# Emptying the q and k banks of attention with ScalarE alone, and splitting them from SBUF

## The chip, the cores and the metric

The kernel runs on one core of a Trainium2 chip. Its engines are TensorE (PE, with the weight load PEld beside it), VectorE (DVE), ScalarE (ACT), GpSimd (POOL) and the DMA queues that SyncE (SP) and ScalarE issue to. The metric is the device time of one execution in microseconds, lower is better. The output must agree with the reference.

## What is computed

The reference is an encoder of two layers on 1024 tokens of width 1024. Each layer multiplies the normalised input with one combined matrix and hands the columns to three mixers: a convolution module, differential attention and a gated delta rule. What matters here, cut from it:

```python
h = rms_norm(x, ...)
u = h @ W_in                       # one projection, its columns go to the three mixers
# differential attention: 6 heads, two softmax maps for each
qf = q.reshape(..., 2 * H, 32) * 32 ** -0.5
s  = einsum("bqmd,bkmd->bmqk", qf, kf)
p  = softmax(s - slopes * |t - s|)
a  = p[:, :, 0] - lam * p[:, :, 1]
# gated delta rule, in chunks of 64
A   = where(strict, (kb @ k^T) * decay, 0)
sol = triangular_solve(A, rhs, lower=True, unit_diagonal=True)
y = concat(A, B, C) @ W_out ;  x = x + rms_norm(y)
x = x + rms_norm(relu(rms_norm(x) @ W1)^2 @ W2)
```

## The kernel before

**Products.** Every dense product in fp32 is made from three matmuls of a rounded type (mm3, L163 to L165): each operand is held as a high part (the value rounded) and a low part (the rest), and high*high, high*low and low*high are summed in a PSUM bank. `split` makes the parts from a tile in SBUF: ScalarE copies it to the high part (L168), VectorE subtracts that from the tile (L169). `load_split` loads a slice of a weight by SP (L177) and splits it (tiles wr, wh, wl).

**The stage.** In each layer the product with W_in runs as a list of column slices, `dense_fm` for each: 128 columns by 1024 tokens, as two halves of 512 tokens, each half 24 matmuls into one of three banks named at, and then a function that empties the bank. `dense_fm` runs that function under a high priority. `attqk(w, j)` is the slice of attention's q (w = 0) or k (w = 1), pair j of three: ScalarE writes the high part qkh from the bank (L425 with the scale for q, L428 for k), and VectorE the low part qkl from the bank and qkh (L426, L429). Then three DMAs of 512 KB write them to DRAM (L434): two of qkh from ScalarE's queue, one of qkl from SP's. There are 2 layers x 2 x 3 = 12 calls, and 24 halves.

**Beside it** runs the delta rule's triangular inverse, `invert`, once for each p = 0, 1, 2 in a layer, as a generator of which pieces are woven into the list of slices. SP loads the blocks (tiles Lr and Lp, L776), ScalarE transposes half of them (L777), GpSimd does 31 steps of substitution, a product and a difference in each (L787 to a tile subt, L788 to Xm), ScalarE transposes the result (L790, XT), SP stores it to xi (L792, L793) and loads its blocks (Ta and Tt, L801, L804), and PE makes the blocks off the diagonal from them (L811, L819). The results (kta) are stored and loaded again for the scan. VectorE in the meantime does the convolution (L508, L512, accumulators ca), and small parts of the delta rule.

**The stage behind** is attention, with the scan woven in. Its first matmuls (L1068) take a stack of q and k that SP loads from DRAM (tile stkE, L1038, three loads), then that of the next block (stk).

**The order** of each engine's instructions is set when the kernel is built: the program gives the operations and their priorities, and a scheduler that estimates when each could run puts them in a row, engine by engine. A change of one operation therefore also moves others. At run time each engine works through its row in order and waits where an operand isn't there.

Of the kernel before, what the change touches and what calls it, by code (L numbers as in the profile page):

```python
# [9 lines left out]
F32 = mybir.dt.float32  # L10
F32R = mybir.dt.float32r
BF16 = mybir.dt.bfloat16
AF = mybir.ActivationFunctionType
ALU = mybir.AluOpType
# [64 lines left out]
class K:  # L79
# [213 lines left out]
    def w_in_phase(self, l, L):  # L293
        nc, a, tc = self.nc, self.a, self.tc
        win = a["w_in"][l].rearrange("(c p) n -> p c n", p=P)
        hTh, hTl = self.hT
        with tc.tile_pool(name=f"wA{l}", bufs=1, reuse_waits=RW) as W:

            def tmp(name, dt=F32, n=S):
                return W.tile([P, n], dt, tag="tmp", bufs=self.TB, name=name)  # L300
# [83 lines left out]
            with tc.tile_pool(name=f"gt{l}", bufs=1, side="right", reuse_waits=RW) as gp:  # L384
                ps = self.rot_bank()[:, 0:NT * 48].rearrange("p (t x) -> p t x", x=48)
# [30 lines left out]
            def attqk(w, j):  # L416
                col = (C_DQ, C_DK)[w] + j * P
                th = tmp(f"qkh{l}_{w}_{j}", F32R)
                tl = tmp(f"qkl{l}_{w}_{j}", F32R)
                qs = self.C["qs"][:, j:j + 1]  # L420

                def ev(n, ps):
                    sl = slice(512 * n, 512 * n + 512)
                    if w == 0:
                        nc.scalar.activation(th[:, sl], ps, AF.Copy, scale=qs)  # L425
                        nc.vector.scalar_tensor_tensor(tl[:, sl], ps, qs, th[:, sl].bitcast(F32), ALU.mult, ALU.subtract)  # L426
                    else:
                        nc.scalar.activation(th[:, sl], ps, AF.Copy)  # L428
                        nc.vector.tensor_tensor(tl[:, sl], ps, th[:, sl].bitcast(F32), op=ALU.subtract)  # L429

                self.dense_fm(win[:, :, col:col + P], ev)
                for b in range(3):
                    lo = b == 2 - (w == 0)
                    (nc.sync if lo else nc.scalar).dma_start(self.qk[j, b, :, w], (tl if lo else th).bitcast(F32))  # L434
# [13 lines left out]
            for j in range(3):  # L448
                todo += [lambda j=j: attqk(0, j), lambda j=j: attqk(1, j)]
# [1185 lines left out]
```

## Time and profile before

| | us |
|---|---|
| median of 3 runs | 2913.32 |
| lowest and highest | 2912.23, 2919.48 |
| the profiled execution | 2917.9 |
| its span in the trace | 2916.1 |

The stages in the trace: the product with W_in of layer 0, then from 409.04 us on attention and the scan, then the product with W_out and the MLP; layer 1 repeats this, with its attention from 1864.51 us on. A row of a timeline reads: start, duration, engine, line, operation, output <- inputs, shape, and in brackets how long the engine was idle before it and what ended that.

### The profile page before, as it was taken

What the parts mean: (1) busy time and instruction counts of PE and PEld (TensorE: products, weight loads), DVE (VectorE), ACT (ScalarE), POOL (GpSimd) and SP (SyncE); (2) the same over time, 40 slices, a digit from 0 to 9 for tenths busy, and PEclk for the clock granted to TensorE, in tenths of its full rate; (3) what the DMA queues carried; (4) which work ended last, traced back from release to release, by engine and by line L of the source; (5) the groups of instructions that cost most, each with busy time, mean ns of one, the idle gap of its engine ahead of it and who ended that gap; (6) DMA issues with size and microseconds to landing.
All of it is one profiled execution on the core that took longest, in us unless ns stands there. A gap on an engine that the chain in (4) does not pass through costs nothing.

```text
span 2916.1 us, 46184 instructions
## 1 busy us (share of the span) xinstructions
PE 2681.5 (92%) x17292; PEld 2155.4 (74%) x17292; DVE 2064.0 (71%) x3781; ACT 1404.8 (48%) x2468; POOL 842.7 (29%) x793
## 2 busy tenths in 40 slices
PE   8987989888999998999999879698889999989997
PEld 7865766666888886888787667476668888868886
DVE  5797247987488776777768871388874977757776
ACT  5433336586356664322554332276853566643224
POOL 2289636754100000000112985377530000000000
PEclk9998989989999999999999989799989999999999
DMA  5467795433235558655445496953332455586643
GB/s 133 151 172 210 219 225 145 117 102 123 87 105 216 206 192 314 233 202 184 150 118 146 142 265 170 224 150 107 109 121 75 145 196 206 212 336 209 220 169 116
DMA packets 415314, 504.76 MB, mean 173 GB/s; under 512 B 125401, under 2 KB 313945, under 8 KB 412786
## 3 DMA queue, kind: packets, MB, share of 16 engines
q1 hardware_dynamic: 359362, 373.92, 42.9%
q10 hardware_dynamic: 55728, 127.88, 11.5%
q8 instruction: 137, 2.24, 0.3%
q14 instruction: 87, 0.71, 0.1%
HBM read 318.01 MB, written 182.12 MB: 172 GB/s over the span
## 4 chain that ended last, share of the span: by engine, by line
PE 62%; POOL 11%; DMA 10%; DVE 8%; issue 4%; ACT 2%; SPq 2%; ACTq 0%; DVEq 0%; POOLq 0%
PE at L163 10%; PE at L164 10%; PE at L165 10%; PE sc L163 4%; PE sc L164 4%; PE sc L165 4%; POOL Xm L788 4%; POOL subt L787 3%; DVE sc L1070 3%; PE dt L163 2%; PE dt L164 2%; PE dt L165 2%; PE tr L163 2%; PE tr L164 2%; DMA qkT<-gq 2%
## 5 line engine op out<-in xcount | busy, mean ns | idle before, releaser
L158 POOL TENSOR_TENSOR pro<-pr,mhalf 128x1 f32<-128x1 f32 x32 | 18.5, 578 | 1417.8 <-DVE pr L207 1415.0
L163 PE MATMUL at<-hTh,wh 128*128 128x512 f32 (+1 forms) x832 | 326.8, 394 | 11.8 <-DVE qkl L426 8.0
L165 PE MATMUL at<-hTh,wl 128*128 128x512 f32 (+1 forms) x832 | 325.5, 392 | 5.4 <-DVE wl L169 5.4
L164 PE MATMUL at<-hTl,wh 128*128 128x512 f32 (+1 forms) x832 | 326.3, 392 | 0.0
L1073 ACT ACTIVATE sc<-sc,mx 128x1024 f32<-128x1024 f32 x192 | 220.2, 1149 | 94.3 <-DVE mx L1070 89.1
L163 PEld LDWEIGHTS at<-hTh,wh 128*128 128x128 f32 x832 | 160.3, 193 | 43.4 <-DVE qkl L426 8.5
L165 PEld LDWEIGHTS at<-hTh,wl 128*128 128x128 f32 x832 | 160.3, 193 | 37.2 <-DVE wl L169 6.2
L164 PEld LDWEIGHTS at<-hTl,wh 128*128 128x128 f32 x832 | 160.6, 193 | 31.0 <-issue 0.8
L1068 PE MATMUL at<-stk 96*128 96x512 f32 x352 | 153.7, 489 | 29.7 <-DVE mx L1070 27.9
L1070 DVE CUSTOM_DVE_ANT_0 sc<-at,bias 128x512 f32<-128x512 f32 x192 | 129.7, 684 | 43.0 <-PE at L1068 25.0
L1070 DVE CUSTOM_DVE_ANT_0 sc<-at,bias,mx 128x512 f32<-128x512 f32 x192 | 141.9, 745 | 19.6 <-PE at L1068 13.8
L1180 ACT ACTIVATE ob<-sb 128x512 fp32r<-128x512 f32 x120 | 74.8, 626 | 155.0 <-PE tr L165 54.8
L169 DVE TENSOR_TENSOR wl<-wr,wh 128x1024 fp32r<-128x1024 f32 x48 | 65.2, 1359 | 117.5 <-ACT wh L168 117.4
L787 POOL TENSOR_TENSOR subt<-Lp,Xm 128x31 f32<-128x31 f32 (+15 forms) x186 | 124.9, 672 | 70.9 <-DMA Lp<-ai 50.5
L163 PE MATMUL at<-ob,oa 128*128 128x512 f32 x356 | 138.4, 391 | 2.1 <-ACT at L1508 2.1
L164 PE MATMUL at<-ob,oa 128*128 128x512 f32 x356 | 138.6, 390 | 0.0
L165 PE MATMUL at<-ob,oa 128*128 128x512 f32 x356 | 138.0, 389 | 0.0
L788 POOL TENSOR_TENSOR Xm<-Xm,subt 128x31 f32<-128x31 f32 (+15 forms) x186 | 133.9, 720 | 12.9
L1094 PE MATMUL tr<-consts,sc 128*128 128x128 f32 x704 | 114.8, 296 | 15.3 <-DVE sc L1090 4.6
L1180 ACT ACTIVATE ob<-w2r 128x512 fp32r<-128x512 f32 x92 | 57.6, 629 | 130.7 <-PE tr L165 52.1
L1094 PEld LDWEIGHTS tr<-consts,sc 128*128 128x128 f32 x704 | 85.7, 150 | 36.9 <-issue 11.4
L1068 PEld LDWEIGHTS at<-stk 96*128 96x128 f32 x352 | 66.0, 203 | 61.2 <-DVE mx L1070 48.9
(469 smaller groups left out, 7940.2 us busy)
## 6 DMA issues: line engine op xcount, KB each, us to landing
hd<-oa ACTq DMA_DIRECT2D x120, 512.0 KB, 6.3
oa<-hd SPq DMA_DIRECT2D x120, 512.0 KB, 4.4
w1r<-in_w_ff_dram SPq DMA_DIRECT2D x32, 1024.0 KB, 5.6
w2r<-in_w_ff_dram SPq DMA_DIRECT2D x64, 512.0 KB, 7.1
wr<-in_w_in_dram SPq DMA_DIRECT2D x50, 512.0 KB, 4.8
ld<-hd SPq DMA_DIRECT2D x98, 256.0 KB, 3.9
kta<-kta SPq DMA_DIRECT2D x32, 576.0 KB, 9.9
stk<-qk SPq DMA_DIRECT2D x66, 256.0 KB, 5.0
```

Source lines behind the costliest of these rows:

```text
L158: self.nc.gpsimd.tensor_tensor(out, x, half[:, :n], op=ALU.pow)
L163: mm(ps, lhsT=lh, rhs=rh, start=first, stop=False, skip_group_check=more)
L164: mm(ps, lhsT=lh, rhs=rl, start=False, stop=False, skip_group_check=more)
L165: mm(ps, lhsT=ll, rhs=rh, start=False, stop=last, skip_group_check=more)
L169: (eng or self.nc.vector).tensor_tensor(lo, raw, hi.bitcast(F32), op=ALU.subtract)
L787: nc.gpsimd.tensor_tensor(tv, Lp[:, j + 1:, j:j + 1].broadcast_to([P, n, w]), Xm[:, j:j + 1, 0:w].broadcast_to([P, n, w]), op=ALU.mult)
L788: nc.gpsimd.tensor_tensor(Xm[:, j + 1:, 0:w], Xm[:, j + 1:, 0:w], tv, op=ALU.subtract)
L1068: mm(ps, lhsT=st[:, 0, t * P:(t + 1) * P], rhs=st[:, 1, ks], start=True, stop=True)
L1070: nc.vector.tensor_tensor_reduce(out=sc[:, ks], in0=ps, in1=self.bias[:, o:o + 512], scale=slope, scalar=mx[:, 0:1] if n2 else 3.0e38, op0 ...
L1073: nc.scalar.activation(sc, sc, AF.Exp, scale=-1.0, bias=mx[:, 1:2], accum_out=oS[:, t, mp:mp + 1])
L1094: nc.tensor.transpose(ps[:, k], pp[0][:, (4 * q + k) * P:(4 * q + k + 1) * P], self.ident)
L1180: self.nc.scalar.activation(h, src, AF.Copy)
```

## The change

`attqk` no longer writes both parts from the bank. ScalarE copies each half to the tile qkl as plain fp32 (with the scale for q), and that is all that reads the bank. Behind the two halves, outside of the high priority, `split` is called on the whole tile: ScalarE makes qkh from qkl in SBUF (L168, 128x1024), and VectorE overwrites qkl with qkl minus qkh (L169, 128x1024). The DMAs stand behind that.

```diff
 def ev(n, ps):
     sl = slice(512 * n, 512 * n + 512)
-    if w == 0:
-        nc.scalar.activation(th[:, sl], ps, AF.Copy, scale=qs)
-        nc.vector.scalar_tensor_tensor(tl[:, sl], ps, qs, th[:, sl].bitcast(F32), ALU.mult, ALU.subtract)
-    else:
-        nc.scalar.activation(th[:, sl], ps, AF.Copy)
-        nc.vector.tensor_tensor(tl[:, sl], ps, th[:, sl].bitcast(F32), op=ALU.subtract)
+    nc.scalar.activation(tl[:, sl].bitcast(F32), ps, AF.Copy, scale=1.0 if w else qs)

 self.dense_fm(win[:, :, col:col + P], ev)
+self.split(tl.bitcast(F32), th, tl)
 for b in range(3):
```

`split`, which it calls, is unchanged:

```python
def split(self, raw, hi, lo, eng=None):
    self.nc.scalar.activation(hi, raw, AF.Copy)
    (eng or self.nc.vector).tensor_tensor(lo, raw, hi.bitcast(F32), op=ALU.subtract)
```

The scheduler moves other instructions too, in the latter part of each W_in stage and in both attention stages; the MLP keeps its order. Three places follow. The changed kernel's line numbers are four lower behind the edit. A name such as Lp0_2 is layer 0, p = 2; qkl0_0_2 is layer 0, q, pair 2.

ScalarE's row in layer 0, from the transpose behind p = 1 (XT0_1) to that ahead of p = 2 (Lp0_2), before:

```order
L790 ACTIVATE XT0_1_1729<-Xm0_1_1728 128x1024
L537 ACT_TABLE_LOAD
L537 ACTIVATE yo0_0_3033<-sc1133_3011,conv_ln_b_347,conv_ln_w_345 128x256 x2
L538 DMA yd_76<-yo0_0_3033 128x256 x2
L425 ACTIVATE qkh0_0_2_3187<-at149_3222,consts_63 128x512
L168 ACTIVATE wh153_3319<-wr153_3318 128x1024
L434 DMA qk_75<-qkh0_0_2_3187 128x1024 x2
L777 ACTIVATE Lp0_2_2377<-Lr0_2_2376 64x1024
```

and in the changed kernel:

```order
L786 ACTIVATE XT0_1_1729<-Xm0_1_1728 128x1024
L533 ACT_TABLE_LOAD
L533 ACTIVATE yo0_0_3033<-sc1133_3011,conv_ln_b_347,conv_ln_w_345 128x256 x2
L534 DMA yd_76<-yo0_0_3033 128x256 x2
L168 ACTIVATE wh153_3319<-wr153_3318 128x1024
L424 ACTIVATE qkl0_0_2_3188<-at149_3221,consts_63 128x512
L168 ACTIVATE qkh0_0_2_3187<-qkl0_0_2_3188 128x1024
L430 DMA qk_75<-qkh0_0_2_3187 128x1024 x2
L773 ACTIVATE Lp0_2_2377<-Lr0_2_2376 64x1024
```

One more copy of 128x1024 stands ahead of the transpose, and the two DMAs of qkh are issued behind it.

SP's queue in layer 1, between p = 1 and p = 2 (xi1 is where p = 1 is stored, Lr1_2 the blocks that p = 2 starts from, wr1735 a weight slice), before:

```order
L792 DMA xi1_80<-Xm1_1_15135 128x1024
L793 DMA xi1_80<-XT1_1_15136 128x1024
L177 DMA wr1735_16945<-in_w_in_dram 128x8x128
L776 DMA Lr1_2_15783<-ai0_77 16x32x32 x4
L646 DMA vs_83<-vs1_1_1_15843 128x4x128
L434 DMA qk_75<-qkl1_0_2_16595 128x1024
```

and in the changed kernel:

```order
L788 DMA xi1_80<-Xm1_1_15135 128x1024
L772 DMA Lr1_2_15783<-ai0_77 16x32x32 x2
L177 DMA wr1735_16945<-in_w_in_dram 128x8x128
L789 DMA xi1_80<-XT1_1_15136 128x1024
L772 DMA Lr1_2_15783<-ai0_77 16x32x32 x2
L430 DMA qk_75<-qkl1_0_2_16595 128x1024
```

Two of the four loads of Lr now stand ahead of the store of XT and of the weight slice.

SP's queue in layer 0 at the start of attention (stkE0 is the first stack of q and k, stk0_0_1 the second, vtE0 the first block of v), before:

```order
L1038 DMA stkE0_3384<-qk_75 32x2048 x3
L476 DMA vtE0_3385<-av_74 128x1024
L743 DMA eg0_2_3693<-eg_85 64x3x128
L1038 DMA stk0_0_1_4303<-qk_75 32x2048 x3
L743 DMA eg0_2_3693<-eg_85 64x3x128
```

and in the changed kernel:

```order
L1034 DMA stkE0_3384<-qk_75 32x2048
L1034 DMA stk0_0_1_4303<-qk_75 32x2048 x3
L1034 DMA stkE0_3384<-qk_75 32x2048 x2
L472 DMA vtE0_3385<-av_74 128x1024
L739 DMA eg0_2_3693<-eg_85 64x3x128 x2
```

The three loads of the second stack now stand between the first load and the last two of the first stack.

## Rows read from the trace of the kernel before

**Rows 1.** The page: busy time of each engine, and shares of the chain by engine.

```profile
PE 2681.5 (92%) x17292; PEld 2155.4 (74%) x17292; DVE 2064.0 (71%) x3781; ACT 1404.8 (48%) x2468; POOL 842.7 (29%) x793
...
PE 62%; POOL 11%; DMA 10%; DVE 8%; issue 4%; ACT 2%; SPq 2%; ACTq 0%; DVEq 0%; POOLq 0%
```

**Rows 2.** Tile qkl: who waited for it (us, times), in the whole execution.

```profile
  PE at L163: 8.0, 1
```

**Rows 3.** Timeline of PE: two places in layer 0's W_in stage, and the first attention matmuls.

```profile
230.89 0.80 PE L163 MATMUL at<-hTh,wh 128*128 128x512 f32 x1 [8.05 <-DVE qkl L426]
...
236.29 0.31 PE L811 MATMUL dt<-Ta,Ao 32*32 32x32 f32 x2 [3.75 <-DMA Ta<-xi]
...
409.04 1.19 PE L1068 MATMUL at<-stkE 96*128 96x512 f32 x2 [6.65 <-DMA stkE<-qk]
...
415.65 0.73 PE L1068 MATMUL at<-stk 96*128 96x512 f32 x2
```

**Rows 4.** Timeline of ScalarE: layer 0 at 227 and 301 us, layer 1 at 1755 us.

```profile
227.27 1.97 ACT L790 ACTIVATE XT<-Xm 128x1024 f32<-128x1024 f32 x1 [15.42 <-POOL Xm L788]
229.14 0.68 ACT L425 ACTIVATE qkh<-at,consts 128x512 fp32r<-128x512 f32 x1
...
301.07 1.05 ACT L168 ACTIVATE wh<-wr 128x1024 fp32r<-128x1024 f32 x1
...
303.36 2.12 ACT L777 ACTIVATE Lp<-Lr 64x1024 f32<-64x1024 f32 x1 [1.23 <-DMA Lr<-ai]
...
1755.08 2.11 ACT L777 ACTIVATE Lp<-Lr 64x1024 f32<-64x1024 f32 x1 [2.35 <-DMA Lr<-ai]
```

**Rows 5.** Timeline of VectorE: layer 0's W_in stage, five places.

```profile
230.10 0.74 DVE L426 SCALAR_TENSOR_TENSOR qkl<-at,consts,qkh 128x512 fp32r<-128x512 f32 x1
...
248.09 1.51 DVE L169 TENSOR_TENSOR wl<-wr,wh 128x1024 fp32r<-128x1024 f32 x1
...
314.24 1.22 DVE L169 TENSOR_TENSOR wl<-wr,wh 128x1024 fp32r<-128x1024 f32 x1 [6.77 <-ACT wh L168]
315.98 0.68 DVE L429 TENSOR_TENSOR qkl<-at,qkh 128x512 fp32r<-128x512 f32 x1
...
325.53 1.65 DVE L169 TENSOR_TENSOR wl<-wr,wh 128x1024 fp32r<-128x1024 f32 x1 [4.19 <-ACT wh L168]
```

**Rows 6.** Timeline of GpSimd: the substitution at the same places, and layer 1's at 1766 us.

```profile
247.70 0.82 POOL L787 TENSOR_TENSOR subt<-Lp,Xm 128x156 f32<-128x156 f32 x1
248.60 1.36 POOL L788 TENSOR_TENSOR Xm<-Xm,subt 128x156 f32<-128x156 f32 x1
...
305.61 0.26 POOL L787 TENSOR_TENSOR subt<-Lp,Xm 128x31 f32<-128x31 f32 x1 [0.68 <-ACT Lp L777]
...
314.29 1.63 POOL L788 TENSOR_TENSOR Xm<-Xm,subt 128x207 f32<-128x207 f32 x1
...
316.00 0.60 POOL L787 TENSOR_TENSOR subt<-Lp,Xm 128x220 f32<-128x220 f32 x1
...
324.69 0.69 POOL L788 TENSOR_TENSOR Xm<-Xm,subt 128x255 f32<-128x255 f32 x1
...
326.17 1.60 POOL L788 TENSOR_TENSOR Xm<-Xm,subt 128x256 f32<-128x256 f32 x1
...
1766.50 0.60 POOL L788 TENSOR_TENSOR Xm<-Xm,subt 128x207 f32<-128x207 f32 x1
```

**Rows 7.** Timeline of SP, the time to issue: attention's start, and Lr in layer 1.

```profile
396.09 3.29 SPq L1038 DMA_DIRECT2D stkE<-qk  x3
...
401.93 3.72 SPq L1038 DMA_DIRECT2D stk<-qk  x3
...
1746.84 4.83 SPq L776 DMA_DIRECT2D Lr<-ai  x4
```

**Rows 8.** Windows of attention: PE, PEld, DVE, ACT, POOL busy, then clock, DMA share, GB/s.

```profile
409.00:500.00 91.00, 82.19 (x997) 60.87 (x999) 68.98 (x185) 59.89 (x114) 52.43 (x38) 0.91 0.69 176
500.00:600.00 100.00, 90.38 (x1080) 68.58 (x1077) 89.80 (x229) 63.86 (x125) 65.00 (x44) 0.91 0.41 106
```

## The prediction

> **What bounds the kernel now.** I read the page first: PE is busy 92% of the span and holds 62% of the chain, but GpSimd, busy 29%, holds 11% [rows 1]. A chain that leaves the busiest engine is where a small change can count, so the next view was the chain in order of time. In the tail of each W_in stage, which is where the twelve calls of `attqk` stand, it runs through GpSimd's substitution (L787, L788), from there to ScalarE's transposes (L790, L777), to SP's stores and loads, and so to the first stack of attention. PE has slack there: the first attention matmul of layer 0 waits 6.65 us for stkE [rows 3]. So a microsecond that PE gains in this tail is worth nothing, and one that the substitution or SP's queue loses is paid. Then I asked who waits for what the change removes (rows 2), and looked at what runs at the same time on VectorE and GpSimd (rows 5 and 6).
>
> **The wait that goes.** The edit takes VectorE out of the release of 24 banks. In the whole execution PE waits for VectorE's eviction once, for 8.0 us [rows 2], at 230.89 us [rows 3]. But VectorE is not why: ScalarE had waited 15.42 us for the substitution to be done, transposed it until 229.24, and only then wrote qkh, until 229.82; VectorE read the bank at 230.10 and was done at 230.84 [rows 4, 5]. With the edit PE starts at about 229.9, 1.0 us earlier. Three matmuls later it stops again, for 3.75 us, on Ta [rows 3], which comes from SP and not from the banks; in the changed row of PE that wait still stands three dense matmuls behind. So the 1.0 us goes into the next wait: **0**, at most -1.0. Nobody else waits for these evictions.
>
> **ScalarE's new copies.** Twelve copies of 128x1024 at 1.05 us (the nearest row is the same operation on a weight, from SBUF to SBUF [rows 4]) are 12.6 us; the 24 evictions stay at about their 0.68. ScalarE is busy 48% [rows 1], and these copies wait for nothing that is late, so most is hidden by idle time. The exception is layer 0 between p = 1 and p = 2: the order shows one copy more ahead of L777, which starts at 303.36 behind the copy of 301.07 and its DMAs [rows 4], and GpSimd starts p = 2 as soon as L777 is through [rows 6]. L777 had waited 1.23 us for Lr, but the copy and two issues behind it end at about 304.6: **+1.2** (between 0 and +1.2: the lower end if the eviction ahead of it comes sooner). That is also what a cover gone would cost elsewhere: 1.05 us a copy.
>
> **VectorE's own time.** 24 operations of 0.74 (q, 12) and 0.68 (k, 12) go [rows 5], 17.0 us. Twelve of L169 come; undisturbed one takes 1.22, among GpSimd's work 1.51 to 1.65 [rows 5], so 14.6 to 19.8 us. That is nothing either way, and what waits for it, a store of qkl, isn't wanted before attention begins: stkE is issued at 396.09 [rows 7].
>
> **What the new form does to GpSimd.** This is the main term. L169 reads two tiles in SBUF; L426 and L429 read one and a bank. In the trace the two kinds differ in what they do to the operation of GpSimd beside them:
> - with the L169 of 314.24, L788 on 128x207 takes 1.63; the same shape takes 0.60 in layer 1, where VectorE is idle [rows 5, 6]: 1.03 more;
> - with that of 325.53, 128x256 takes 1.60; its neighbour of 128x255 takes 0.69: 0.91 more;
> - in p = 1, where VectorE's convolution (two tiles in SBUF as well) already holds GpSimd up, with that of 248.09 an operation takes 1.36 against 0.82 for its neighbour: 0.54 more;
> - beside L429 at 315.98, L787 on 128x220 takes 0.60: nothing more [rows 5, 6].
>
> So operations free for GpSimd become ones that hold it. By the order, nine of the twelve splits fall on a substitution: four on p = 1 and one on p = 2 in layer 0, three and one in layer 1. At 0.54 for the seven in p = 1 and 0.95 for the two in p = 2 this is 3.8 + 1.9 = **+5.7**. The bounds are 0, if the splits land in the gaps in which GpSimd waits, and 9 x 1.03 = +9.3. I take the rows of the stage that each split lies in.
>
> The Trainium skill speaks against the change here: its page "SBUF — State Buffer", section "Who interferes with whom", says that a VectorE instruction with two SBUF inputs contends with a GpSimd instruction that reads SBUF, one with at most one such input doesn't, and that the lock is exclusive. The trace agrees on who contends (1.63 against 0.60); if GpSimd stood still for the whole of each split, the sum would be that of the first rival below.
>
> **What is moved on SP.** Layer 1, before p = 2: L777 waits 2.35 us for Lr [rows 4], whose four loads take 4.83 us to issue [rows 7]. Two of them now stand ahead of XT's store, in time in which SP waited for ScalarE, so the rest ends up to 2.4 us sooner; ScalarE's row has L777 earlier too. **-2.0**, between -2.4 and 0. Layer 0, at attention's start: three loads of the second stack, 3.72 us of issuing [rows 7], stand ahead of two of the first. The first attention matmul, which waits for stkE [rows 3], can be up to 3.7 later, but the second stack, wanted at 415.65 [rows 3], is then there already, and the scheduler's store ahead of it on ScalarE comes earlier. **+1.0**, between 0 and +3.7, nearer the lower end since PE's work behind the second stack catches up.
>
> **Attention's order.** Both attention stages are reordered as a side effect, with the same operations. No row prices this. VectorE is busy 68.98 of 91.00 us at the start of layer 0's attention, and 89.80 of 100.00 later [rows 8], so the start holds (0.898 - 0.758) x 91 = 12.7 us of idle time more than steady work does. A better order could win back at most that much, and a worse one lose about as much as SP's term above, 3.7 a layer. I take **0**, as the same work meets the same bound.
>
> **The sum.** -0 (bank) + 1.2 (ScalarE) + 5.7 (GpSimd) - 2.0 + 1.0 (SP) + 0 (order) = +5.9 us. The profiled execution of 2917.9 would become 2923.8; it lies 4.6 above the median, 2913.3, and the comparison is with the median: 2913.3 + 5.9 = **2919**.
>
> **Rivals.**
> 1. *The lock is dearer.* If GpSimd stands still for a whole split, each of the nine costs an average of the 1.22, 1.51 and 1.65 seen [rows 5], 1.46: 13.1 instead of 5.7, so +13.3, **2927**. For it: 1.03 was lost with a split of 1.22. Against it: 0.91 with one of 1.65. It decides the sign that can be measured from (8.7 - 0.2) / 9 = 0.94 us a split on. The rule of the Trainium skill's page "SBUF — State Buffer" would give this.
> 2. *The start of attention gets faster.* Its new order fills VectorE's extra idle time, 12.7 us in layer 0 [rows 8], with none counted for layer 1: -12.7, and +0.2 for the tail's other terms with the splits in gaps, **2901**. For it: attention begins with stacks that come late [rows 3], and the order of loads there has changed. Against it: nothing in the edit makes them come sooner.
> 3. *The change doesn't do what it says.* The banks were released late by ScalarE's queue and not by VectorE [rows 4], so nothing is gained; and the splits land in GpSimd's gaps, so nothing is lost: **2913**. For it: one wait in the whole execution [rows 2]. Against it: GpSimd has few gaps in p = 1.
>
> **How the numbers follow.** About 0.3%, 8.7 us, is what a measurement of this kernel can tell from no change. My forecast, +5.9, with its own range of 2911 to 2927, has 0.40; of that 0.12 lies above 2922. Rival 1 has 0.20, all of it slower. Rival 2 has 0.28, of which 0.04 within the bound. Rival 3 has 0.12. So faster 0.24, same 0.28 + 0.04 + 0.12 = 0.44, slower 0.12 + 0.20 = 0.32. The range for 8 in 10 reaches from 2902, which leaves out about 0.12 of rival 2, to 2931, which is rival 1 with SP's two terms at their upper ends and leaves out under 0.08.
>
> **What would show it.** In the changed trace: no wait of PE for tile qkl, and a wait of about 7 us at the same place, now for ScalarE (the bank step); GpSimd operations beside an L169 on qkl longer by 0.5 to 1.0 us, p = 1 and p = 2 longer by 2.2 and 0.9 us in layer 0 (the main term); GpSimd's p = 2 starting 1.2 us later after the end of p = 1 in layer 0 and 2 us sooner in layer 1; the first attention matmul of layer 0 some 5 us later than 409.04. I am wrong if the substitutions keep their lengths, or if attention itself, from its first matmul to the last, changes by more than 4 us in either layer: then the order and not the edit made the time.

## The result and the profile after

The change makes the kernel slower. Four runs of it have a median of 2935.7 us (2931.75 to 2941.1) against 2914.94 for four of before (2912.23 to 2919.48). The two medians are 20.8 us apart; the ratio on record, 1.0065 with a 95% interval of [1.0048, 1.0082], makes it some 19 us, and that is what is used below. The forecast was 2919, and 2935.7 lies above the range of 2902 to 2931. The profiled execution of the changed kernel took 2941.1 us, with a span of 2939.3; that is 23.2 more than the span before. Line numbers of the changed kernel are four lower behind the edit, so that L1066 there is L1070 of before.

The page's busy times, and its chain by engine, to be read against [rows 1]:

```profile
PE 2688.7 (91%) x17292; PEld 2160.6 (74%) x17292; DVE 2080.8 (71%) x3769; ACT 1417.8 (48%) x2480; POOL 852.8 (29%) x793
...
PE 63%; DMA 10%; POOL 10%; DVE 9%; issue 4%; ACT 2%; SPq 1%; ACTq 0%; DVEq 0%; POOLq 0%
```

The counts are as the diff says: 12 operations fewer on VectorE, 12 more on ScalarE. But VectorE is busy 16.8 us longer, where 17.0 us of evictions went out and at most 19.8 came in: 14 us more than the edit's own, so some other work of VectorE got longer.

Where the time appears is seen on PE. Its first attention matmul is at 417.02 in layer 0 (409.04 before, [rows 3]) and at 1874.49 in layer 1 (1864.51 before); the transposes that end attention are at 719.65 (709.32) and 2182.49 (2157.33). So the changed kernel is 8.0 us late when attention of layer 0 begins, 10.3 when it ends, 10.0 when attention of layer 1 begins and **25.2 when that ends**. Layer 1's attention alone is 15.2 us longer, though it holds the same operations. The windows of it, of before and then of after (length, busy us of PE, PEld, DVE, ACT and POOL with their counts, granted clock, DMA share, GB/s):

```profile
1864.51:2157.33 292.82, 257.62 (x2752) 189.83 (x2753) 248.08 (x625) 200.75 (x390) 186.25 (x113) 0.92 0.43 120
```

```profile
1874.49:2182.49 308.00, 262.85 (x2753) 194.56 (x2753) 261.99 (x625) 201.76 (x390) 188.41 (x113) 0.91 0.42 115
```

VectorE does the same 625 operations in 262.0 instead of 248.1 us. PE is not busy for 45.2 us instead of 35.2. What it waits for there stands in the view of PE's waits (engine, line, what it waited for: us in total, times, longest), of before and then of after:

```profile
PE at L1068 <- DVE mx L1070: 11.7, 15, 5.0
...
PE tr L1094 <- POOL sc L1088: 3.6, 1, 3.6
```

```profile
PE at L1064 <- DVE mx L1066: 19.9, 24, 3.5
...
PE tr L1090 <- POOL sc L1084: 8.7, 3, 4.2
```

Both are attention's own. The first (L1070 of before) is VectorE emptying a bank of scores and taking their minimum (tile mx). The second (L1088) is GpSimd adding the two softmax maps of a block, behind which PE transposes the sum. Neither is touched by the diff; they are in another order.

### The profile page after: what moved, and what is told of

Its sections match the earlier page's. It is cut to its first block, busy times and chain, and to the rows that moved or that the text cites. A ratio compares the mean times of both kernels' runs of the same rounds, so it can differ in the third digit from the quotient of the medians.

```text
span 2939.3 us, 46177 instructions
## 1 busy us (share of the span) xinstructions
PE 2688.7 (91%) x17292; PEld 2160.6 (74%) x17292; DVE 2080.8 (71%) x3769; ACT 1417.8 (48%) x2480; POOL 852.8 (29%) x793
## 4 chain that ended last, share of the span: by engine, by line
PE 63%; DMA 10%; POOL 10%; DVE 9%; issue 4%; ACT 2%; SPq 1%; ACTq 0%; DVEq 0%; POOLq 0%
PE at L163 10%; PE at L164 10%; PE at L165 10%; PE sc L163 4%; PE sc L164 4%; PE sc L165 4%; POOL Xm L784 4%; POOL subt L783 3%; DVE sc L1066 2%; PE dt L163 2%; PE dt L164 2%; PE dt L165 2%; PE tr L1090 2%; PE at L1064 2%; PE tr L163 2%
## 5 line engine op out<-in xcount | busy, mean ns | idle before, releaser
L1066 DVE CUSTOM_DVE_ANT_0 sc<-at,bias 128x512 f32<-128x512 f32 x192 | 130.0, 685 | 49.0 <-PE at L1064 38.9
L1066 DVE CUSTOM_DVE_ANT_0 sc<-at,bias,mx 128x512 f32<-128x512 f32 x192 | 142.2, 746 | 20.7 <-PE at L1064 15.5
L169 DVE TENSOR_TENSOR wl<-wr,wh 128x1024 fp32r<-128x1024 f32 x48 | 63.7, 1327 | 125.0 <-ACT wh L168 125.0
L1090 PE MATMUL tr<-consts,sc 128*128 128x128 f32 x704 | 117.6, 300 | 28.0 <-POOL sc L1084 18.4
L1090 PEld LDWEIGHTS tr<-consts,sc 128*128 128x128 f32 x704 | 87.9, 152 | 49.5 <-POOL sc L1084 20.6
L1094 ACT ACTIVATE aT<-tr 128x512 f32<-128x512 f32 x160 | 91.9, 592 | 59.2 <-PE tr L1090 59.0
```

Of the source, the lines that this page charges most:

```text
L169: (eng or self.nc.vector).tensor_tensor(lo, raw, hi.bitcast(F32), op=ALU.subtract)
L1066: nc.vector.tensor_tensor_reduce(out=sc[:, ks], in0=ps, in1=self.bias[:, o:o + 512], scale=slope, scalar=mx[:, 0:1] if n2 else 3.0e38, op0 ...
L1090: nc.tensor.transpose(ps[:, k], pp[0][:, (4 * q + k) * P:(4 * q + k + 1) * P], self.ident)
L1094: nc.scalar.activation(aT[:, 4 * q:4 * q + 4, qi * P:qi * P + P], ps, AF.Copy)
```

## The experiments

The edit and the order come together, so most experiments hold one still. To do that, every engine's row is fixed by links between neighbours, from a table of the program's instructions; the links add no wait at run time, since each engine works through its row in order anyway (e5_att1_sp below, which has all the tables in and differs from before in SP's row of one stage alone, measures 0.9990). The function, and its use:

```diff
+def _pin(tc, nc, table, shift=0):
...
+        for p, q in zip(row, row[1:]):
+            tc.add_manual_dep(ins[q + shift], ins[p + shift].name, mybir.DependencyInfo(mybir.DependencyClass.NoSync, mybir.DependencyReason.DATA), reason="pin")
...
         tile_hybrid_encoder_kernel(tc, args, out)
+        _pin(tc, nc, PIN0, 0)
```

There are six tables, PIN0 to PIN5, one for each stretch (per layer: W_in, attention, the rest). Below, a comment behind a call says whose order the table holds; calls that keep the order which the kernel has anyway are left out. A ratio is to before on the same chip, with its 95% interval; "+9.9 us" is that ratio less one, times before's median there (2915 to 2920 us); it lies up to 4 us off the difference of the two medians, and the interval reaches some 3 to 5 us to either side (7 to 8 for e4_changed_again and e4_oldatt_halfpool).

### The edit apart from the order

**e1_edit_oldatt**: the changed kernel, with both attention stages in the order of before.

```diff
+        _pin(tc, nc, PIN4, 0)  # layer 0's attention: order of before
+        _pin(tc, nc, PIN5, 0)  # layer 1's attention: order of before
```

> The changed kernel, with every engine's order in both attention stages put back to that of the kernel before (chains of same-engine dependencies, no waits added), and its own order everywhere else. In the trace of the changed kernel attention takes 302.6 us in layer 0 (before: 300.3) and 308.0 in layer 1 (before: 292.8). Theory 1, the order of attention alone costs this: both stages go back to 300.3 and 292.8, so about 17.5 us less than the changed kernel, a median of 2918. Theory 2, attention is slower because of what the edit leaves it (stacks of q and k that arrive later or otherwise): the stages stay at 302.6 and 308.0, median 2935.

Measured: 1.0034 [1.0019, 1.0049], +9.9 us. Layer 1's attention takes 291.61 us, against 292.82 before and 308.00 after. About half of the 19 us is gone.

**e1_noedit_newatt**: the kernel before, with both attention stages in the changed order. No instruction of the program differs from before.

```diff
+        _pin(tc, nc, PIN4, 0)  # layer 0's attention: changed order
+        _pin(tc, nc, PIN5, 0)  # layer 1's attention: changed order
```

> The kernel before, without the edit, with every engine's order in both attention stages taken from the changed kernel, and its own order everywhere else. Theory 1 (order): attention takes 302.6 and 308.0 us though nothing was edited, and the median is 2914.9 + 17.5 = 2932. Theory 2 (edit): attention takes 300.3 and 292.8 as before, median 2915.

Measured: 1.0035 [1.0018, 1.0053], +10.2 us. The order of attention alone, without the edit, costs about what undoing it gave back in the run before.

**e1_edit_oldall**: the edit with the order of before everywhere; the 24 copies stand where ScalarE's evictions stood, and only the twelve splits, which before doesn't have, are placed by the scheduler.

```diff
+        _pin(tc, nc, PIN0, 0)  # and PIN1 to PIN5: order of before
```

> The changed kernel with every instruction that both kernels have in the order of the kernel before, in all stages; only the 12 pairs of the new split find their own places. This is the edit without its reordering. By the sum of my prediction without its terms of order (ScalarE +1.2, GpSimd held up by the new two-input operations +5.7, nothing from the order on SP or in attention): 2915 + 7 = 2922, with the substitutions longer by some 0.5 to 1.0 us for each split that falls on them. If the new operations don't hold GpSimd up: within 2 us of the kernel before, 2915. If attention is slower by the edit itself: 2932 or more.

Measured: 1.0016 [1.0000, 1.0032], +4.7 us. This is the price of the edit itself, though its interval just touches 0.

**e3_noedit_newwin** and **e4_noedit_newall**: the kernel before with the changed order in the W_in stages alone, and then in all stages.

```diff
+        _pin(tc, nc, PIN0, 0)  # and PIN1, layer 0's and layer 1's W_in: changed order
```

```diff
+        _pin(tc, nc, PIN0, 0)  # and PIN1 to PIN5: changed order
```

> The kernel before, without the edit, with every engine's order in both W_in stages taken from the changed kernel, and its own order elsewhere. By difference of two runs (the edit with the new order outside attention +9.9 us, the edit in the old order everywhere +4.7) the tail's new order should cost 5 us by itself: attention of layer 0 begins 3 us later after the end of p = 2 since the second stack's loads stand among the first's, and the median is 2921. If that order costs only together with the split's operations in it: 2916.

> The kernel before, without the edit, in the changed kernel's order in all stages. Attention's order alone took +10.2 us and that of the W_in stages alone +1.5: if they add up, +12, 2928; if the new W_in order costs only where the split's operations stand in it, the same +10 to +12; if the two orders fit each other and either is only bad against the other's old one, clearly under +10, 2920.

Measured: 1.0005 [0.9987, 1.0024], +1.5 us, and 1.0042 [1.0025, 1.0059], +12. The first was expected at +5; W_in's order alone can't be told from nothing. But e1_edit_oldatt less e1_edit_oldall, 9.9 - 4.7, says that the same order costs 5 us when the edit is there. The intervals of the two overlap, and I leave it at 1.5 to 5.

**e4_changed_again**: the changed kernel once more without any edit, to see the spread between two profiles of one kernel.

> The changed kernel as it is, for a narrower interval of the whole effect (+18.9 us from four runs). If the parts add up as measured so far, edit in the old order +4.7, its own order in the W_in stages about +5, its order in attention about +10: +20, a ratio of 1.0068 within 0.002. If the parts overlap, less: 1.005.

Measured: 1.0067 [1.0045, 1.0090]. Layer 1's attention takes 303.0 here, 5 less than in the first profile, but PE's wait for mx is 20.5 and for the map sum 6.3: the waits repeat better than the stage's length does. In layer 0 the length tells nothing: attention there takes 295 to 306 us in the profiles of all runs that have the old order in it, and 297 to 307 in the four that have the changed one.

So the 19 us are the edit at 4.7, the order of attention at 10 and W_in's order at 1.5 to 5, each known to some 5 us.

### What the edit costs: the subtraction beside GpSimd

**e3_oldall_nosub** and **e3_oldall_twice** are e1_edit_oldall with VectorE's subtraction cut to one column (so the low parts of q and k are left unmade), and with the subtraction done twice (so the low parts are wrong by qkh).

```diff
-self.split(tl.bitcast(F32), th, tl)
+nc.scalar.activation(th, tl.bitcast(F32), AF.Copy)
+nc.vector.tensor_tensor(tl[:, 0:1], tl[:, 0:1].bitcast(F32), th[:, 0:1].bitcast(F32), op=ALU.subtract)
```

```diff
 self.split(tl.bitcast(F32), th, tl)
+nc.vector.tensor_tensor(tl, tl.bitcast(F32), th.bitcast(F32), op=ALU.subtract)
```

> The edit in the old order (as e1_edit_oldall), with VectorE's subtraction of each split cut from 1024 columns to one, so that the low parts are not made; ScalarE's copies stay. In e1_edit_oldall the substitutions p = 1 and p = 2 take 59.71 and 43.79 us in layer 0 and 60.16 and 42.82 in layer 1, before 57.24, 42.81, 57.79, 42.67. Lock theory (a VectorE operation with two tiles in SBUF holds GpSimd up): they go back to 57.2, 42.8, 57.8 and 42.7 within 0.4, and the median falls from +4.7 to about 0 or +1 against the kernel before. Rival (ScalarE's twelve new copies and their DMAs do it): they stay at 59.7 and 60.2, and the median at +5.

> The edit in the old order (as e1_edit_oldall), with VectorE's subtraction of each split done twice in a row, so that the low parts are wrong; nothing else differs. Lock theory: the second subtraction costs the substitution under it about what the first did, 2.5 us on p = 1 and up to 1 on p = 2 in each layer: p = 1 at 62 us in both layers, and a median of +4.7 + 5 = +10 against the kernel before, 2926. Rival (the subtractions cost nothing, something else in the edit does): p = 1 stays at 60, the median at +5.

Measured: 0.9992 [0.9976, 1.0008], -2.3 us, and 1.0044 [1.0027, 1.0061], +12.8. So from none to one subtraction is 7 us and from one to two 8 us, for an operation that PE waits for 0.4 us at most, and once. GpSimd pays most of it. Its first and its last operation of the substitution p = 1 in layer 0, from the timelines of e1_edit_oldall, e3_oldall_nosub and e3_oldall_twice:

```profile
237.32 0.48 POOL L783 TENSOR_TENSOR subt<-Lp,Xm 128x31 f32<-128x31 f32 x1
...
296.78 0.25 POOL L784 TENSOR_TENSOR Xm<-Xm,subt 128x31 f32<-128x31 f32 x1
```

```profile
238.55 0.48 POOL L784 TENSOR_TENSOR subt<-Lp,Xm 128x31 f32<-128x31 f32 x1
...
294.32 0.25 POOL L785 TENSOR_TENSOR Xm<-Xm,subt 128x31 f32<-128x31 f32 x1
```

```profile
238.09 0.48 POOL L784 TENSOR_TENSOR subt<-Lp,Xm 128x31 f32<-128x31 f32 x1
...
301.24 0.25 POOL L785 TENSOR_TENSOR Xm<-Xm,subt 128x31 f32<-128x31 f32 x1
```

From first start to last end these are 59.71, 56.02 and 63.40 us; before it is 57.24. With p = 1 and p = 2 of both layers together, e1_edit_oldall has 59.71 + 43.79 + 60.16 + 42.82 = 206.5, before 57.24 + 42.81 + 57.79 + 42.67 = 200.5, e3_oldall_nosub 195.9 and e3_oldall_twice 212.3. Without the subtraction p = 1 lies 1.2 to 1.6 us below before; why, no run shows. The old evictions are not seen to have held GpSimd up (0.60 beside one of them, [rows 6]), but other work beside p = 1 moved too: four splits of weights fall on it in layer 0 before, three in e3_oldall_nosub.

A rival that these runs leave in place is SP's queue: the store of qkl stands in it behind the subtraction, with loads behind the store. SP's waits for the subtraction, in e1_edit_oldall, e3_oldall_nosub and e3_oldall_twice (before has 3.2 and 1.9 us for the two evictions):

```profile
SPq L430 <- DVE qkl L169: 12.2, 3, 7.1
```

```profile
SPq L431 <- DVE qkl L428: 9.5, 2, 6.4
```

```profile
SPq L431 <- DVE qkl L428: 22.2, 4, 11.2
```

From none to one the substitutions grow by more (10.6 us) than the whole does (7), and SP's wait by 2.7; from one to two they grow by less (5.8 of 8), and SP's wait by 10. So GpSimd accounts for the first, and the second may in part be SP's.

One meeting of such a subtraction with the substitution, from the timelines of VectorE and of GpSimd in the changed kernel:

```profile
315.31 1.23 DVE L169 TENSOR_TENSOR wl<-wr,wh 128x1024 fp32r<-128x1024 f32 x1 [2.72 <-ACT wh L168]
316.45 1.55 DVE L169 TENSOR_TENSOR qkl<-qkl,qkh 128x1024 fp32r<-128x1024 f32 x1
```

```profile
315.37 1.54 POOL L783 TENSOR_TENSOR subt<-Lp,Xm 128x175 f32<-128x175 f32 x1
316.99 1.39 POOL L784 TENSOR_TENSOR Xm<-Xm,subt 128x175 f32<-128x175 f32 x1
318.46 0.56 POOL L783 TENSOR_TENSOR subt<-Lp,Xm 128x192 f32<-128x192 f32 x1
319.09 0.59 POOL L784 TENSOR_TENSOR Xm<-Xm,subt 128x192 f32<-128x192 f32 x1
```

Each of the two splits, a weight's and the new one, lengthens the operation of GpSimd beside it, to 1.54 and 1.39 us where the larger one of 128x192, with VectorE idle, takes 0.59. The ends tell more than the lengths: the new split is done at 318.00 and GpSimd's operation 0.38 us later, at 318.38; and the split itself, 1.55 instead of 1.23, ends 1.09 us behind GpSimd's operation before (316.91). So each stands still until the other's instruction is through, and the length of a split beside GpSimd holds the split's own wait.

### Where attention's order loses

**e2_att0_as_att1**: layer 0's attention in the order that layer 1's has before, to see whether one order is the better for both.

```diff
+        _pin(tc, nc, PIN4, 0)  # layer 0's attention: layer 1's order of before
```

> The kernel before, without the edit; layer 0's attention in the order that layer 1's attention has (the two stages consist of the same 2288 instructions), all else in its own order. In the trace before, attention takes 300.3 us in layer 0 and 292.8 in layer 1. If the order sets that difference: layer 0's attention takes about 293, and the median falls by some 7 us to 2908. If what layer 0 starts from sets it (loads that come later): no change, 2915, or slower where the order doesn't suit.

Measured: 1.0010 [0.9993, 1.0027]. Layer 0's attention takes 300.2 us, as before (300.3); the gain that I expected isn't there.

**e5_att1_sp**, **e5_att1_pool**, **e5_att1_engines**: the kernel before, with the changed order in layer 1's attention only: on SP's queue; on GpSimd; on PE, ScalarE, VectorE and GpSimd, but not on SP. Other mixes have engines that wait on each other in a circle.

```diff
+        _pin(tc, nc, PIN5, 0)  # layer 1's attention: changed order on SP; GpSimd; all but SP
```

> The kernel before, without the edit; of the changed kernel's order only SP's queue in layer 1's attention (26 of its 95 loads stand elsewhere: those of the scan's chunk 6 ahead of the stacks of pair 3), all else old. If SP's loads cost the 10 us: from the end of p = 2 to the end of attention 367 us and a median 10 over the kernel before. If the other engines' order costs it: 357 us, no change.

> The kernel before, without the edit; of the changed kernel's order only GpSimd's in layer 1's attention (46 of its 90 operations stand elsewhere), all else old. If it is which of GpSimd's operations stand beside VectorE's that costs: VectorE busy about 260 us in that stage (old 246) and up to 10 us more. If GpSimd's order costs only with that of PE, ScalarE and VectorE: VectorE at 246 to 250 and no change within 3 us.

> The kernel before, without the edit; the changed kernel's order of PE, ScalarE, VectorE and GpSimd in layer 1's attention, SP's and all else old. If the engines' order costs: VectorE busy 260 us, 367 us from the end of p = 2 to the end of attention, +10 against the kernel before. If SP's: 357 us and no change.

Measured: 0.9990 [0.9974, 1.0006], 1.0076 [1.0058, 1.0093] and 1.0036 [1.0018, 1.0055]. SP's order is worth nothing. GpSimd's row alone costs 22 us, twice what all the engines together cost (10.5); it may be that the other rows of the changed order are in step with GpSimd's. Its windows, and PE's waits in it:

```profile
1867.25:2179.90 312.65, 259.38 (x2752) 191.32 (x2753) 245.53 (x625) 201.48 (x390) 188.30 (x113) 0.91 0.42 113
```

```profile
PE tr L1094 <- POOL sc L1088: 14.0, 3, 5.6
PE at L1068 <- DVE mx L1070: 12.9, 11, 6.7
```

PE waits 14.0 us for map sums, 3.6 before; VectorE, at 245.5 us, is not slower than before. What differs in GpSimd's row begins so, in the kernel before and then in the changed one (sc is a block's map, Sg, kta and qkT belong to the scan):

```
L1087 TENSOR_TENSOR sc1870_18499<-sc1870_18499,cf1_1_1_18526 128x1024
L1088 TENSOR_TENSOR sc1867_18490<-sc1867_18490,sc1870_18499 128x1024
L848 TENSOR_TENSOR Sg1_8_17818<-Sb1_1_16854,eg1_4_17584 128x384 x2
L1125 TENSOR_TENSOR sq1_0_18318<-oatt1_0_17727 128x512
L753 TENSOR_TENSOR kta1_5_17848<-kta1_5_17848,kw1_13716 128x384
```

```
L844 TENSOR_TENSOR Sg1_8_17818<-Sb1_1_16854,eg1_4_17584 128x384 x2
L1083 TENSOR_TENSOR sc1870_18499<-sc1870_18499,cf1_1_1_18526 128x1024
L1121 TENSOR_TENSOR sq1_0_18318<-oatt1_0_17727 128x512
L749 TENSOR_TENSOR kta1_5_17848<-kta1_5_17848,kw1_13716 128x384
L1084 TENSOR_TENSOR sc1867_18490<-sc1867_18490,sc1870_18499 128x1024
```

The sum of map 1867 now stands behind a multiplication of the scan, which waits for its load. Five more of the stage's 20 sums are likewise put behind operations of the scan. The same place in the timeline of e5_att1_pool, GpSimd and then PE:

```profile
1949.76 1.16 POOL L753 TENSOR_TENSOR kta<-kta,kw 128x384 f32<-128x384 f32 x1 [4.16 <-DMA kta<-kta]
1950.88 2.33 POOL L1088 TENSOR_TENSOR sc<-sc,sc 128x1024 f32<-128x1024 f32 x1
```

```profile
1953.27 1.12 PE L1094 MATMUL tr<-consts,sc 128*128 128x128 f32 x4 [5.65 <-POOL sc L1088]
```

GpSimd waits 4.16 us for kta's load with a sum behind it in its row, and PE, which needs the sum, 5.65.

Three runs test this reading (each says in its own text what its letters stand for). **e6_pool_sumsfirst** keeps the changed row of GpSimd but for the map sums, which stand ahead of the scan's operations again; **e6_pool_first** makes the first of the moves alone, on the row of before; **e6_pool_rest** makes the others.

```diff
+        _pin(tc, nc, PIN5, 0)  # layer 1's attention, GpSimd: changed row with the sums moved up; first move alone; the other moves
```

> The kernel before; in layer 1's attention GpSimd has its changed row, the one that alone cost 22 us, but each map sum (L1087, L1088) stands again ahead of those operations of the scan and of the norm that it stands ahead of in the old row. Every other engine keeps its old row. Theory A (PE is late because map sums stand behind operations of the scan that wait for their loads): the 22 us are gone, 0 to +4 us. Theory B (the other moves in GpSimd's row, of the scan and the norm against each other, cost the time): +15 us or more is left.

> The kernel before; in layer 1's attention one move on GpSimd alone: the sum for map sc1867 (L1087, L1088) stands behind two L848 of the scan and behind kta's multiplication (L753), which waited 4.2 us for its load in the run of the whole changed row. Theory A: about 4 us for the wait and 1 to 2 us for the operations passed, +3 to +6 us. Theory B, or PE has slack there: within 2 us.

> The complement of the run before: that first move is left out, and GpSimd has the rest of its changed row in layer 1's attention, with five more map sums behind operations of the scan. Theory A: the 22 us less what the first move costs alone, so +14 to +20 us. If one early wait were all that counts, within 4 us.

Measured: 1.0026 [1.0014, 1.0037], +7.6 us; 1.0017 [1.0005, 1.0029], +5.0; 1.0049 [1.0034, 1.0064], +14.3. The first move alone costs about what its wait is worth, and with the others makes 19 of the 22; both lie where the reading puts them. Moving the sums back takes away 14 of the 22, less than the 18 to 22 that I expected. What is left is, in its profile, not a wait. The windows of e6_pool_sumsfirst:

```profile
1866.45:2166.11 299.66, 263.68 (x2752) 194.74 (x2753) 245.31 (x625) 201.89 (x390) 188.97 (x113) 0.90 0.43 118
```

PE is idle for 36.0 us, as before (35.2; 53.3 with the whole changed row), so its waits are all mended; but it is busy 263.7 instead of 257.6, at a mean granted clock of 0.90 instead of 0.92 of its 2.4 GHz. e1_edit_oldall, in the order of before, shows a like profile (261.4 at 0.90), and e5_att1_engines (264.1) and e6_new_twofirst (268.6) have 0.89. Why the clock was lower in these, no run tells, nor whether the 7.6 us that are left belong to GpSimd's row at all.

**e6_new_twofirst**: the changed order on all engines in layer 1's attention, with the first two late sums put back.

```diff
+        _pin(tc, nc, PIN5, 0)  # layer 1's attention: changed order, sums of maps 1867 and 1887 moved up
```

> The kernel before with the changed order of all engines in layer 1's attention only, and two of GpSimd's map sums (sc1867, sc1887) put back ahead of the operations of the scan; the others can't be put back there, since engines would wait on each other in a circle. The changed order of both layers costs 10.2 us, nearly all of it in this stage. Theory A: 2 of 6 late sums are mended, so 3 to 6 of the 10 us come back, +4 to +7. Theory C (VectorE's 13 to 15 us of longer work in that order make the time): VectorE stays at 260 us and the run at +8 to +12.

Measured: 1.0050 [1.0034, 1.0065], +14.6 us. Nothing comes back: PE waits 9.7 us for sums and 19.2 for mx. So the reading that holds for GpSimd's row alone isn't shown for the whole changed order; that a mended sum meets rows there that are laid out for a late one would be a reason, but no run tests it.

What all the engines' order has beside late sums is VectorE. **e3_newatt_halfpool** and **e4_oldatt_halfpool** halve GpSimd's two operations on the maps (half of the columns are left uncombined), in the changed and in the old order, to see whether it is their time on GpSimd that holds VectorE up.

```diff
-nc.gpsimd.tensor_tensor(pp[1], pp[1], cf[:, 1, qi:qi + 1].broadcast_to([P, S]), op=ALU.mult)
+nc.gpsimd.tensor_tensor(pp[1][:, :512], pp[1][:, :512], cf[:, 1, qi:qi + 1].broadcast_to([P, 512]), op=ALU.mult)
...
-self.lastpool = nc.gpsimd.tensor_tensor(pp[0], pp[0], pp[1], op=ALU.add)
+self.lastpool = nc.gpsimd.tensor_tensor(pp[0][:, :512], pp[0][:, :512], pp[1][:, :512], op=ALU.add)
...
+        _pin(tc, nc, PIN5, 0)  # and layer 0's attention: changed order; order of before
```

> The kernel before, without the edit, with the changed kernel's order in attention (as e1_noedit_newatt, which takes 306.6 and 300.8 us in the two attention stages, 10.2 us over the kernel before), and GpSimd's own operations on the attention maps (L1087, L1088) cut to half of their columns; the other half is left out. Lock theory (VectorE's two-input operations wait for those of GpSimd): the 29 operations of L1090 in layer 1's attention fall from 54.7 us towards 29 x 1.28 = 37, to below 46, all of VectorE's work there from 299.8 to below 291, and the two stages to below 300 and 294, so the median falls by 12 us or more, to 2915 or less. Rival (the new order costs by waits between the engines, whatever GpSimd does beside VectorE): L1090 stays at about 54 and the median at 2926.

> The kernel before in its own order throughout, with GpSimd's operations on the attention maps (L1087, L1088) cut to half of their columns, the other half left out: the control to e3_newatt_halfpool, which took 2901.5, 15.5 us less than the kernel before. Lock theory: with GpSimd's operations halved, most of what the new order cost (10.2 us) is gone, so the old order gains less from the cut than the new one did: 2897 to 2901, within 5 us of e3_newatt_halfpool. Rival (the new order costs by something other than GpSimd's operations beside VectorE's): the 10 us between the orders stay, 2891.

Measured: 0.9947 [0.9929, 0.9964] and 0.9884 [0.9857, 0.9910]. With that work halved the two orders are still (0.9947 - 0.9884) x 2916 = 18 us apart, where I expected at most 5; VectorE's difference in layer 1's attention shrinks from 14 us to 245.5 - 239.9 = 5.6. So the long work of VectorE goes with GpSimd's maps, but the time that the order costs doesn't go with it.

Layer 1's attention in all these runs, from windows and waits (PE's rest is the length less its busy time):

| order of layer 1's attention | length | PE's rest | PE for mx | PE for sums | VectorE busy |
|---|---|---|---|---|---|
| before (before, e1_edit_oldatt, e1_edit_oldall, e2_att0_as_att1, e5_att1_sp) | 292 to 298 | 34 to 39 | 8.4 to 13.0 | 0.2 to 4.5 | 245 to 248 |
| changed (after, e4_changed_again, e1_noedit_newatt, e4_noedit_newall) | 301 to 308 | 42 to 45 | 18.3 to 20.8 | 5.9 to 8.7 | 260 to 262 |
| changed but for SP (e5_att1_engines) | 309 | 45 | 14.7 | 15.0 | 254 |
| changed on GpSimd alone (e5_att1_pool) | 313 | 53 | 12.9 | 14.0 | 246 |
| the same, sums moved up (e6_pool_sumsfirst) | 300 | 36 | 11.7 | 4.4 | 245 |
| all changed, two sums moved up (e6_new_twofirst) | 313 | 44 | 19.2 | 9.7 | 257 |

In the changed order PE waits some 9 us more for mx and 4 more for sums in the mean of its four profiles. PE's rest as a whole is 7.5 us longer (35.7 to 43.1), since other waits are shorter, and PE is busy 2.4 longer; together that is the 10 us. The cause of a late sum is shown for the row of GpSimd alone, and is not shown for the whole order.

## Why the prediction was wrong

The steps, in the order of the prediction:

- **The bank, -0.** Right. PE's wait for qkl at this place was 8.05 and is 7.04, for ScalarE now, as said; and 0.8 of the 1.0 us is lost again three matmuls on, where the wait for Ta grows from 3.75 [rows 3] to 4.52. PE in the changed kernel:

```profile
229.20 0.80 PE L163 MATMUL at<-hTh,wh 128*128 128x512 f32 x1 [7.04 <-ACT qkl L424]
...
235.38 0.31 PE L807 MATMUL dt<-Ta,Ao 32*32 32x32 f32 x2 [4.52 <-DMA Ta<-xi]
```

- **ScalarE, +1.2.** The place was right, the size was not: from the end of p = 1 to the start of p = 2 in layer 0 it is 12.43 us, 10.09 before, +2.3. The copy stood ahead of L773, as the order said, and the two DMAs of qkh behind the copy were not issued at once:

```profile
304.09 1.06 ACT L168 ACTIVATE qkh<-qkl 128x1024 fp32r<-128x1024 f32 x1
306.69 0.81 ACTq L430 DMA_DIRECT2D qk<-qkh  x2
307.67 2.08 ACT L773 ACTIVATE Lp<-Lr 64x1024 f32<-64x1024 f32 x1 [2.52 <-DMA vT<-gq]
```

  The copy ends at 305.15 and the DMAs are issued from 306.69 on, 1.5 us later, which I hadn't counted; the trace puts the wait down to a load of vT. In the old order (e1_edit_oldall) the gap is 10.77, +0.7.
- **GpSimd's lock, +5.7.** The total is right, the price of a split in p = 1 is not: in the old order the four substitutions are 206.5 - 200.5 = 6.0 us longer together, and the changed kernel's own are 59.60 + 43.39 + 59.51 + 43.87 = 206.4. But in the changed trace eight of the nine splits cost the operation beside them 0.86 to 0.99 us each, in p = 1 as in p = 2 (the ninth falls on other work of GpSimd). The 0.54 for p = 1 was 1.36 less a neighbour of 0.82 [rows 6] that had been held up itself: the same shape takes 0.50 undisturbed.

```profile
314.79 0.50 POOL L784 TENSOR_TENSOR Xm<-Xm,subt 128x156 f32<-128x156 f32 x1
```

  Nine at some 0.9 would be 8; that the total is 6 all the same, with other work beside the substitutions moved, is luck. The whole edit in the old order costs 4.7 [0.0, 9.3], where its terms in the sum were 1.2 + 5.7. The first rival, 13.1 for these nine, falls as a price: it took a split's length, 1.22 to 1.65, and what is over 1.22 in it is the split's own wait for GpSimd (the one of 248.09 is through at 249.60, 1.08 us behind the end of GpSimd's 247.70, [rows 5, 6]). The rule behind it does not fall. The Trainium skill's page "SBUF — State Buffer" has VectorE with two inputs in SBUF contend with a GpSimd instruction that reads SBUF (section "Who interferes with whom"), and calls the pair of ports that they share exclusive and held for the full instruction (section "Terms"). The trace agrees on who contends (1.39 beside the split, 0.56 and 0.59 behind it) and on how long: GpSimd's operation ended 0.38 us behind the split.
- **SP in layer 1, -2.0.** Wrong: the gap between p = 1 and p = 2 there is 13.73 us, 13.91 before. The loads of Lr were issued earlier, the last 5.2 us behind the end of p = 1 (1754.62) instead of 8.3. But ScalarE's transpose started 6.4 us behind that, before 3.4 [rows 4, 7], and the trace still puts its wait down to Lr:

```profile
1757.87 1.90 SPq L772 DMA_DIRECT2D Lr<-ai  x2
...
1766.14 2.08 ACT L773 ACTIVATE Lp<-Lr 64x1024 f32<-64x1024 f32 x1 [5.56 <-DMA Lr<-ai]
```

  So what the earlier issue gained, the time to landing lost; why the loads took longer, no run shows.
- **SP in layer 0, +1.0.** The upper end of its 0 to 3.7 was nearer: from the end of p = 2 to the first attention matmul it takes 63.74 us, 60.62 before, +3.1; nearly the same is there without the edit (e3_noedit_newwin, 63.59), though e1_edit_oldall, in the old order, has 62.05 too. The two loads of stkE stand behind those of the second stack, as the order said:

```profile
401.68 0.36 SPq L1034 DMA_DIRECT2D stkE<-qk  x1
404.15 2.68 SPq L1034 DMA_DIRECT2D stk<-qk  x3
406.87 0.89 SPq L1034 DMA_DIRECT2D stkE<-qk  x2
```

  I had set it near the lower end since PE would catch up. That it does isn't seen: layer 0's attention took 302.6 us and 300.3 before, which differ by less than that stage does between profiles of one order.
- **Attention's order, 0. This is the step that failed.** It measures +10 (e1_noedit_newatt, and the difference of the first two runs). Two things were wrong in it. The bounds, -12.7 and +3.7 a layer, were taken from the start of attention, VectorE's idle time and SP's loads [rows 7, 8]; the loss shows in layer 1, which I gave no window of its own. By the times of ScalarE's exponentials it builds up 49 to 94 us behind the start of attention, in all four profiles; but PE waits there for only 4 to 5 us (before: none), and GpSimd does 24 operations there instead of 18, so part of that lag can be other work moved there. And "the same work meets the same bound" took VectorE's work as fixed, though the term of GpSimd's lock in the same sum says that it isn't: what an operation of VectorE takes depends on which one of GpSimd stands beside it. How much of the 10 us this second point makes, no run shows.

The third sign that I named against myself, attention longer by over 4 us in a layer, came out as written (15.2): the order and not the edit made most of the time. The second rival, a faster start of attention, had the wrong sign, and the third, that nothing happens, falls by the 19 us.

What stays open: how the 10 us divide between late map sums and VectorE's longer work, since orders that keep one and mend the other can't all be built, and e6_new_twofirst mended two sums for nothing; and how much of W_in's order (1.5 to 5) belongs to the edit. None of the versions that do all the work is faster than the kernel before beyond its interval.

## What to carry to other kernels

Where a scheduler sets the order, an edit has two prices, and the second one, for stages that the edit doesn't touch, can be the larger: fix the old order, measure the edit alone, then look at which rows moved. On an engine that does two jobs, look at what in its row stands behind an operation that waits for a DMA: a short operation there that another engine needs pays the whole wait. And VectorE work on two SBUF operands is not free because VectorE has time: count whom it stands beside.

## What the runs showed of the hardware

The contention goes both ways. L1090 (two tiles in SBUF, 128x1024) of layer 1's attention, 28 of one form, before and then after (count, busy us, mean ns, idle before it):

```profile
L1090 DVE SCALAR_TENSOR_TENSOR sc<-sc,cf,sc 128x1024 f32<-128x1024 f32 x28 | 42.5, 1533 | 0.4
```

```profile
L1086 DVE SCALAR_TENSOR_TENSOR sc<-sc,cf,sc 128x1024 f32<-128x1024 f32 x28 | 52.3, 1882 | 0.3
```

Some 10 of the 14 us that VectorE loses there are this one line. A single one, in the changed kernel, with what GpSimd does at that time:

```profile
1936.14 2.80 DVE L1086 SCALAR_TENSOR_TENSOR sc<-sc,cf,sc 128x1024 f32<-128x1024 f32 x1
```

```profile
1934.26 3.60 POOL L751 TENSOR_TENSOR qkT<-qkT,eg 128x768 f32<-128x768 f32 x2 [3.08 <-PE dt L881]
1937.82 3.33 POOL L1084 TENSOR_TENSOR sc<-sc,sc 128x1024 f32<-128x1024 f32 x1
```

VectorE takes 2.80 us, its mean before was 1.53; and GpSimd's map sum, 2.33 in e5_att1_pool above, takes 3.33 beside it. VectorE ends at 1938.94, 1.08 us behind GpSimd's operation before (1937.86), as the split above did with 1.09: it had waited for that to end. So what such a meeting costs can't be read off the length of either instruction; the one that came second has its wait in it.
